# Moving rows and outputs of the split matmuls run from the last column to the first

## The chip, the cores and the metric

The kernel runs on one core of one Trainium2 chip. The metric is the time of one execution on the device in microseconds (us); runs before and after are compared by their medians. On this kernel a difference of less than about 0.2% can't be told from none.

## The reference

Two transformer-like blocks follow each other on 256 tokens of width 1024, all in f32. What matters here is that nearly all the work is matrix products of the tokens with weights:

```python
# first block
h = rms_norm(x, norm_mix);  z = h @ w_in              # 1024 -> 7000
#   recurrent branch, gated linear attention, attention over a memory of 256 rows
proj = jnp.einsum("bsnc,ncd->bsnd", branches, w_branch)   # 3 x 768 -> 1024
x = x + jnp.sum(sigmoid(z_gate) * proj, axis=2) @ w_out
up = causal_dwconv(rms_norm(x, norm_ffn) @ w_up, ...)      # 1024 -> 6144
x = x + (gelu(gate_h) * val_h) @ w_down                    # 3072 -> 1024
# second block, on rms_norm(x, final_norm)
u = rmsnorm(x, norm_mix) @ w_in_2                      # attention, state space and pooling mixers
x = x + concat(y_attn, y_ssd, y_pool) @ w_out_2
x = x + (silu(gate) * up) @ w_down_2                   # up, gate: 1024 -> 5632; 2816 -> 1024
return rmsnorm(x, norm_final_2)
```

## The kernel before, in words

**Precision.** An f32 operand is split into two parts, high (`wh`, `xh`) and low (`wl`, `xl`), of type float32r, which TensorE multiplies in one pass. `mm3` makes a product out of three matmuls into the same PSUM tile: high by high (L194), high by low (L195), low by high (L196). Each of them is a weight load (the stationary operand, 128 columns) and a stream of the moving operand (one row in each partition, 256 columns or so) through the array into PSUM.

**Weights.** They come from HBM in the order of `wplan`, a chunk of 1 MB a transfer, three half chunks ahead. ScalarE rounds a half chunk to `wh` (L149), VectorE takes the rest to `wl` (L150). The whole program is written out in this order, with no loop on the chip; element-wise work of other stages is put between the chunks.

**Which operand is stationary.** `chunk_T` (and `down_T`, `last_T` for the first down projection) makes an output that is transposed: weights are stationary, activations (256 tokens) move. A chunk has 256 output columns, which are two tiles of 128; in HBM the columns of the two tiles stand in turn, so a tile's weights are every second float:

```python
c = slice(m, m + nm * (P - 1) + 1, nm)      # chunk_T: nm = 2 tiles, the m-th one
c = (mo // 2) * 2 * P + mo % 2              # pair_cols, for down_T and last_T
return slice(c, c + 2 * P - 1, 2)
```

`chunk_tok` makes an output with tokens in partitions: activations are stationary (128 adjacent columns), weights move (256 columns; 262 or 272 for two chunks). `down_tok` and `last_tok`, the second down projection, do the same with 512 moving columns. Other matmuls with weights in adjacent columns are the 84 of `rg_gate`, the 24 of the narrow chunk xbc3, and the 24 of the scores against the memory.

**Order at the start of a sum.** For the first chunk behind a normalization (wout0, up0, gu0) `chunk_T` is called with `lo_last`: the products with the low part of the activations come last, from L223, since that part is ready last.

Plain f32 matmuls (transposes, the state-space mixer, softmax products) call `pe.matmul` or `pe.transpose` by themselves and not through `mm3`.

Of the kernel before, what the change touches and what calls it, by code (L numbers as in the profile page):

```python
# [17 lines left out]
P = 128  # L18
# [90 lines left out]
def build(ctx: ExitStack, tc: tile.TileContext, ins: dict, out: bass.AP):  # L109
    nc = tc.nc  # L110
    act, dve, pool, pe = nc.scalar, nc.vector, nc.gpsimd, nc.tensor
# [18 lines left out]
    def t2(shape=None, dt=F32):  # L130
        return tp.tile(shape or [P, 512], dt, tag="t2", name=uid("t2"))
# [8 lines left out]
    def bank(shape=None):  # L140
        return psp.tile(shape or [P, 2, 256], F32, tag="ps", name=uid("ps"))
# [45 lines left out]
    def load_w(name, i):  # L187
        q = halves.index((name, i))
        while nxt[0] < min(q + AHEAD + 1, len(halves)):
            emit_half()  # L190
        return loaded.pop((name, i))

    def mm3(o, lh, ll, rh, rl, start, stop, skip=False):
        pe.matmul(o, lh, rh, start=start, stop=False, skip_group_check=skip)  # L194
        pe.matmul(o, lh, rl, start=False, stop=False, skip_group_check=skip)  # L195
        pe.matmul(o, ll, rh, start=False, stop=stop, skip_group_check=skip)  # L196
# [6 lines left out]
    def chunk_T(name, x, nk=KT, nm=2, k_outer=False, lo_last=False):  # L203
        ps = bank()
        for i in range(2):
            wh, wl = load_w(name, i)
            od = [(m, k) for m in range(nm) for k in range(nk // 2)]
            if k_outer:
                od.sort(key=lambda q: q[1])
            for m, k in od:  # L210
                c = slice(m, m + nm * (P - 1) + 1, nm)
                kk = i * (nk // 2) + k
                if lo_last:
                    pe.matmul(ps[:, m, :], wh[:, k, c], x[0][:, kk, :], start=kk == 0 and m == 0,  # L214
                              stop=False, skip_group_check=True)
                    pe.matmul(ps[:, m, :], wl[:, k, c], x[0][:, kk, :], start=False, stop=False,  # L216
                              skip_group_check=True)
                else:
                    mm3(ps[:, m, :], wh[:, k, c], wl[:, k, c], x[0][:, kk, :], x[1][:, kk, :],
                        kk == 0 and m == 0, kk == nk - 1, skip=True)  # L220
            for m, k in od if lo_last else ():
                kk = i * (nk // 2) + k
                pe.matmul(ps[:, m, :], wh[:, k, m:m + nm * (P - 1) + 1:nm], x[1][:, kk, :], start=False,  # L223
                          stop=kk == nk - 1, skip_group_check=True)
        return ps

    def chunk_tok(name, x, nk=KT, wide=False, k_outer=False):

        pss = [bank([P, 512]) for _ in range(2)] if wide else None
        ps = None if wide else bank()  # L230
        for i in range(2):
            wh, wl = load_w(name, i)
            n = wh.shape[2]
            od = [(t, k) for t in range(2) for k in range(nk // 2)]
            if k_outer:
                od.sort(key=lambda q: q[1])
            for t, k in od:
                c = slice(t * P, (t + 1) * P)
                kk = i * (nk // 2) + k
                o = pss[t][:, :n] if wide else ps[:, t, :]  # L240
                mm3(o, x[0][:, kk, c], x[1][:, kk, c], wh[:, k, :], wl[:, k, :],
                    kk == 0 and (wide or t == 0), kk == nk - 1, skip=True)
        return pss if wide else ps
# [94 lines left out]
    m = (mh, ml)  # L338
# [10 lines left out]
    for q in range(4):  # L349
        mem_part(q)  # L350
        for n, name in enumerate(first):
            if q == 0:
                raws[name] = wrp.tile([P, WMAX], F32, tag="raw", name=uid("raw"))
            if q % 2 == 0:
                fw[n] = (whp.tile([P, WMAX // 2], F32R, tag="wh", name=uid("wh")),
                         wlp.tile([P, WMAX // 2], F32R, tag="wl", name=uid("wl")))
            o = WOFF[name][0]
            cr = slice(512 * q, 512 * q + 512)
            c = slice(512 * (q % 2), 512 * (q % 2) + 512)
            nc.sync.dma_start(raws[name][:, cr],  # L360
                              W[o:o + P * 2048].rearrange("(p n) -> p n", p=P)[:, cr])
            split(fw[n][0][:, c], fw[n][1][:, c], raws[name][:, cr])
            for k in range(2):
                for mo in range(2):
                    w0 = c.start + k * 256 + mo
                    cw = slice(w0, w0 + 2 * P - 1, 2)
                    kk = 2 * q + k
                    mm3(fps[n][:, mo, :], fw[n][0][:, cw], fw[n][1][:, cw],
                        mh[:, kk, :], ml[:, kk, :], kk == 0 and mo == 0, kk == KT - 1, skip=True)
# [24 lines left out]

    x_part(0)
    c2 = chunk_T("memk2", m)
    rm = widen(rm_tok, "nA")

# [126 lines left out]
    for j in range(3):  # L525
        ps = chunk_T(f"mq{j}", h)
        if j == 0:
            rx = widen(rx_tok, "nB")
        evac_hl(mq, j, ps, rx)
# [14 lines left out]
    for j in range(3):  # L544
        ps = chunk_T(f"zrnn{j}", h)
        evac_T(zr[:, 2 * j:2 * j + 2, :], ps, rx)
        for f in (2 * j, 2 * j + 1):
            conv_tile(xr[:, f, :], zr[:, f, :], lambda i: pv("rnn_w", 6 * i + f), pv("rnn_b", f), 4)
            split(xrh[:, f, :], xrl[:, f, :], xr[:, f, :])
        step()  # L550
# [50 lines left out]
    for j in range(3):  # L601
        ps = chunk_T(f"qk{j}", h)
# [177 lines left out]
    for j in range(3):  # L780
        ps = chunk_tok(f"v{j}", h, wide=j == 0)
# [22 lines left out]
    for bi, b in enumerate(BR_ORDER):  # L804
# [4 lines left out]
        for j in range(4):  # L809
            ps = chunk_T(f"gate{b}_{j}", h)  # L810
# [3 lines left out]
            o = (outa, outb, outc)[b]  # L814
            ps = chunk_T(f"br{b}_{j}", o, nk=MT)
# [407 lines left out]
    for i, name in enumerate(IN2_ORDER):  # L1223
        if i == 1:
            squares(x2, [sb])
        if name.startswith("vz"):
            ps = chunk_tok(name, h2, wide=i == 0, k_outer=i == 0)
        else:
            ps = chunk_T(name, h2, nm=1 if name == "xbc3" else 2)
# [97 lines left out]
    for t in range(2):  # L1327
        ssq = small([P, 2])
        o = [t2(), t2()]
# [17 lines left out]
        else:  # L1347
            act.activation(o[0], o[0], AF.Copy, scale=r)
            nc.scalar.dma_start(out[rows, 0:512], o[0])
            for i in range(2):  # L1350
                c = slice(256 * i, 256 * i + 256)
# [148 lines left out]
```

## Time and profile before

| | |
|---|---|
| median of 3 runs | 827.11 us (827.09 to 827.94) |
| the profiled execution | 826.78 us, of which 825.0 us are its span, from the first instruction to the last |
| TensorE, matmuls | 814.7 us busy (99%), 6454 instructions |
| TensorE, weight loads | 790.5 us busy (96%), 6454 instructions |
| VectorE | 606.2 us busy (73%) |
| ScalarE | 474.5 us busy (58%) |
| GpSimd | 64.4 us busy (8%) |
| DMA | 144 MB, 175 GB/s on the mean |

Matmuls overlap in TensorE's pipeline, so the busy time says only that TensorE never stood still. What one matmul costs is the distance from its start to the start of the next one.

### The profile page before, as it was taken

How to read it: one execution, taken by the hardware profiler on the slowest of the kernel's cores; microseconds unless marked ns; L12 is line 12 of the kernel's file. 1: busy time of each engine (PE TensorE's matmuls, PEld its weight loads, DVE VectorE, ACT ScalarE, POOL GpSimd, SP SyncE). 2: the span in 40 equal slices, each digit the busy share in tenths (PEclk: the TensorE clock that was granted, in tenths of full speed). 3: DMA queues.
4: the chain of work that ended last, by engine and by line, in shares of the span. 5: the costliest groups of instructions: out<-in, count | busy, mean ns of one | idle time of the engine just before them, and what ended most of it. 6: DMA issues, size and time to landing. Idle time of an engine off the chain costs nothing. (4 is left out here: it accounts for less than half of the span.)

```text
span 825.0 us, 15638 instructions
## 1 busy us (share of the span) xinstructions
PE 814.7 (99%) x6454; PEld 790.5 (96%) x6454; DVE 606.2 (73%) x950; ACT 474.5 (58%) x756; POOL 64.4 (8%) x69
## 2 busy tenths in 40 slices
PE   8999999999999999999999999999999999999996
PEld 8999999999999999999999999999999999999995
DVE  6888757866667677898777787798988756655663
ACT  6845579953445555765555555766966544444443
POOL 2210110000010002000000000207302000000000
PEclk9999999999999999999999999999999999999999
DMA  7774444354345554365555454362163554555521
GB/s 239 292 256 147 167 135 179 124 198 167 129 152 199 195 196 166 126 234 199 172 185 192 168 203 165 116 259 104 60 244 133 215 189 165 196 188 174 201 103 51
DMA packets 23527, 144.04 MB, mean 175 GB/s; under 512 B 2896, under 2 KB 3424, under 8 KB 8480
## 3 DMA queue, kind: packets, MB, share of 16 engines
q1 hardware_dynamic: 22464, 140.98, 48.1%
q0 software_dynamic: 704, 1.80, 0.6%
q8 instruction: 50, 0.82, 0.4%
q10 hardware_dynamic: 288, 0.27, 0.1%
q14 instruction: 21, 0.17, 0.1%
HBM read 141.20 MB, written 1.05 MB: 172 GB/s over the span
## 5 line engine op out<-in xcount | busy, mean ns | idle before, releaser
L150 DVE TENSOR_TENSOR wl<-raw,wh 128x1024 fp32r<-128x1024 f32 (+4 forms) x276 | 329.6, 1201 | 131.6 <-ACT wh L149 128.8
L149 ACT ACTIVATE wh<-raw 128x1024 fp32r<-128x1024 f32 (+4 forms) x276 | 278.5, 1015 | 240.2 <-PE ps L195 182.4
L194 PE MATMUL ps<-H,wh 128*128 128x256 f32 x1320 | 373.7, 283 | 1.4 <-ACT wh L149 1.4
L196 PE MATMUL ps<-H,wl 128*128 128x256 f32 x1320 | 373.7, 283 | 0.2 <-DVE wl L150 0.2
L195 PE MATMUL ps<-H,wh 128*128 128x256 f32 x1320 | 373.1, 283 | 0.0
L194 PEld LDWEIGHTS ps<-H,wh 128*128 128x128 f32 x1320 | 257.5, 195 | 3.7 <-issue 1.6
L195 PEld LDWEIGHTS ps<-H,wh 128*128 128x128 f32 x1320 | 257.0, 195 | 0.3
L196 PEld LDWEIGHTS ps<-H,wl 128*128 128x128 f32 x1320 | 256.3, 194 | 0.4 <-DVE wl L150 0.4
L196 PE MATMUL aux<-S,wl 128*128 128x256 f32 x192 | 54.3, 283 | 0.0
L195 PE MATMUL aux<-S,wh 128*128 128x256 f32 x192 | 54.3, 283 | 0.0
L194 PE MATMUL ps<-wh,H 128*128 128x256 f32 (+2 forms) x192 | 54.2, 282 | 0.0
L196 PE MATMUL ps<-wh,H 128*128 128x256 f32 (+2 forms) x192 | 53.8, 280 | 0.0
L195 PE MATMUL ps<-wl,H 128*128 128x256 f32 (+2 forms) x192 | 53.8, 280 | 0.0
L194 PE MATMUL aux<-S,wh 128*128 128x256 f32 x192 | 53.8, 280 | 0.0
L149 ACT ACTIVATE S<-t 128x256 fp32r<-128x256 f32 x46 | 19.0, 415 | 49.2 <-DVE t L919 25.5
L287 POOL TENSOR_TENSOR t<-t,t 128x512 f32<-128x512 f32 x15 | 21.7, 1448 | 325.6 <-DVE H L153 199.8
L541 DVE SCALAR_TENSOR_TENSOR t<-t,par,t 128x255 f32<-128x255 f32 (+1 forms) x96 | 40.2, 479 | 0.1
L194 PEld LDWEIGHTS aux<-S,wh 128*128 128x128 f32 x192 | 37.4, 195 | 0.0
L195 PEld LDWEIGHTS aux<-S,wh 128*128 128x128 f32 x192 | 37.2, 194 | 0.0
L196 PEld LDWEIGHTS aux<-S,wl 128*128 128x128 f32 x192 | 37.1, 193 | 0.0
L194 PEld LDWEIGHTS ps<-wh,H 128*128 128x128 f32 x192 | 36.1, 188 | 0.4 <-issue 0.4
L196 PEld LDWEIGHTS ps<-wh,H 128*128 128x128 f32 x192 | 36.1, 188 | 0.2
(332 smaller groups left out, 1132.8 us busy)
## 6 DMA issues: line engine op xcount, KB each, us to landing
raw<-w SPq DMA_DIRECT2D x115, 1024.0 KB, 4.8
raw<-w SPq DMA_DIRECT2D x12, 768.0 KB, 4.2
raw<-w SPq DMA_DIRECT2D x12, 256.0 KB, 5.4
raw<-w SPq DMA_DIRECT2D x2, 896.0 KB, 4.5
raw<-w SPq DMA_DIRECT2D x1, 1088.0 KB, 5.0
raw<-w SPq DMA_DIRECT2D x1, 1048.0 KB, 4.8
R<-memT SPq DMA_DIRECT2D x4, 256.0 KB, 5.5
R<-xT SPq DMA_DIRECT2D x2, 512.0 KB, 9.0
```

What stands on the lines that cost most here:

```text
L149: act.activation(dst_h, src, AF.Copy)
L150: dve.tensor_tensor(dst_l, src, dst_h.bitcast(F32), op=ALU.subtract)
L194: pe.matmul(o, lh, rh, start=start, stop=False, skip_group_check=skip)
L195: pe.matmul(o, lh, rl, start=False, stop=False, skip_group_check=skip)
L196: pe.matmul(o, ll, rh, start=False, stop=stop, skip_group_check=skip)
L287: self.eng.tensor_tensor(self.acc, self.acc, sq, op=ALU.add)
L541: dve.scalar_tensor_tensor(dst[:, s:], src[:, :S - s], w(width - 1 - s), dst[:, s:], op0=ALU.mult, op1=ALU.add)
```

## The change

`mm3` and the three matmuls of `chunk_T` that don't go through it read the moving row with step -1 from the last column, and write the output with step -1 from the last column. Output column j is still made from moving column j, so each value lands where it did. Weights, their layout and their loads are the same.

```diff
     def mm3(o, lh, ll, rh, rl, start, stop, skip=False):
+
+        o, rh, rl = (t[:, ::-1] for t in (o, rh, rl))
         pe.matmul(o, lh, rh, start=start, stop=False, skip_group_check=skip)
         pe.matmul(o, lh, rl, start=False, stop=False, skip_group_check=skip)
         pe.matmul(o, ll, rh, start=False, stop=stop, skip_group_check=skip)
...
                 if lo_last:
-                    pe.matmul(ps[:, m, :], wh[:, k, c], x[0][:, kk, :], start=kk == 0 and m == 0,
+                    o, xm = ps[:, m, ::-1], x[0][:, kk, ::-1]
+                    pe.matmul(o, wh[:, k, c], xm, start=kk == 0 and m == 0,
                               stop=False, skip_group_check=True)
-                    pe.matmul(ps[:, m, :], wl[:, k, c], x[0][:, kk, :], start=False, stop=False,
-                              skip_group_check=True)
+                    pe.matmul(o, wl[:, k, c], xm, start=False, stop=False, skip_group_check=True)
...
             for m, k in od if lo_last else ():
                 kk = i * (nk // 2) + k
-                pe.matmul(ps[:, m, :], wh[:, k, m:m + nm * (P - 1) + 1:nm], x[1][:, kk, :], start=False,
+                pe.matmul(ps[:, m, ::-1], wh[:, k, m:m + nm * (P - 1) + 1:nm], x[1][:, kk, ::-1], start=False,
                           stop=kk == nk - 1, skip_group_check=True)
```

All five engines have the same instructions in the same order before and after. In the compiled program a matmul's moving row before has start 0 and step 1, after start 255 and step -1, and so has its output (511 for the wide ones). The weight load of a `chunk_T` tile starts at the tile's last column and has step -2 (two floats), before and after; one with adjacent columns has step -1.

## Rows read from the trace of the kernel before

**Rows 1.** The head of the page: span; busy time, share and instructions of each engine; the granted clock of TensorE in 40 slices, in tenths.

```profile
span 825.0 us, 15638 instructions
PE 814.7 (99%) x6454; PEld 790.5 (96%) x6454; DVE 606.2 (73%) x950; ACT 474.5 (58%) x756; POOL 64.4 (8%) x69
PEclk9999999999999999999999999999999999999999
```

**Rows 2.** The chain of work that ended last, by engine and line, as shares of the span.

```profile
PE 27%; DVE 1%; ACT 0%; issue 0%; DVEq 0%; ACTq 0%
PE ps L196 6%; PE ps L194 6%; PE ps L195 6%; PE aux L196 2%; PE aux L194 2%; PE aux L195 2%; PE ps L223 0%; PE ps L216 0%; PE ps L214 0%; PE aux L1287 0%; PE aux L1017 0%; DVE V L994 0%; DVE V L995 0%; PE aux L1003 0%; DVE t L1203 0%; PE aux L1218 0%
```

**Rows 3.** All waits of TensorE: line waited for, us in total, times, the longest.

```profile
PE ps L194 <- ACT wh L149: 1.4, 1, 1.4
PE aux L1003 <- ACT t L1109: 1.1, 1, 1.1
PE wps L254 <- DVE ones L247: 1.0, 1, 1.0
PE aux L1058 <- DVE V L978: 0.2, 1, 0.2
PE ps L196 <- DVE wl L150: 0.2, 1, 0.2
```

**Rows 4.** Groups of matmuls by line and shape: out<-in by name, rows * weight columns, output shape, count, then busy us and mean ns of one, then idle time before. L519 is plain f32.

```profile
L195 PE MATMUL ps<-H,wh 128*128 128x256 f32 x1320 | 373.1, 283 | 0.0
...
L196 PE MATMUL ps<-wh,H 128*128 128x256 f32 x160 | 44.4, 278 | 0.0
...
L194 PE MATMUL aux<-wh,S 128*128 128x512 f32 x88 | 34.6, 393 | 0.0
...
L519 PE MATMUL aux<-t,M 128*128 128x256 f32 x16 | 4.1, 392 | 0.0
```

**Rows 5.** Timeline of TensorE's matmuls in the first feed-forward (`chunk_T`): start us, duration us.

```profile
300.36 0.28 PE L194 MATMUL ps<-H,wh 128*128 128x256 f32 x1
300.48 0.28 PE L195 MATMUL ps<-H,wh 128*128 128x256 f32 x1
300.60 0.28 PE L196 MATMUL ps<-H,wl 128*128 128x256 f32 x1
300.72 0.28 PE L194 MATMUL ps<-H,wh 128*128 128x256 f32 x1
...
301.08 0.28 PE L194 MATMUL ps<-H,wh 128*128 128x256 f32 x1
...
301.44 0.28 PE L194 MATMUL ps<-H,wh 128*128 128x256 f32 x1
...
301.80 0.28 PE L194 MATMUL ps<-H,wh 128*128 128x256 f32 x1
```

**Rows 6.** Busy time of each engine (and instructions that touch the stretch) in two stretches, the first feed-forward and the wide matmuls at the end: stretch, its length, then PE, PEld, DVE, ACT, POOL, the granted clock, DMA share, GB/s.

```profile
360.00:500.00 140.00, 140.00 (x1169) 140.00 (x1168) 109.99 (x166) 77.32 (x115) 0.00 (x0) 1.00 0.55 194
...
802.00:818.00 16.00, 16.00 (x72) 13.13 (x71) 7.02 (x15) 6.58 (x13) 0.00 (x0) 1.00 0.08 30
```

**Rows 7.** Timeline of matmuls of the memory's values (`chunk_tok`), start and duration in us.

```profile
37.75 0.28 PE L195 MATMUL ps<-wl,H 128*128 128x256 f32 x1
...
38.34 0.28 PE L194 MATMUL ps<-wh,H 128*128 128x256 f32 x1
38.45 0.34 PE L195 MATMUL ps<-wl,H 128*128 128x256 f32 x1
38.63 0.28 PE L196 MATMUL ps<-wh,H 128*128 128x256 f32 x1
...
39.53 0.28 PE L195 MATMUL ps<-wl,H 128*128 128x256 f32 x1
```

**Rows 8.** Timeline of weight loads (PEld) at the start of the kernel, every second float: start and duration in us; in brackets the idle time before and what ended it.

```profile
6.96 0.19 PEld L194 LDWEIGHTS ps<-H,wh 128*128 128x128 f32 x1 [1.58 <-ACT wh L149]
7.08 0.20 PEld L195 LDWEIGHTS ps<-H,wh 128*128 128x128 f32 x1
7.69 0.19 PEld L196 LDWEIGHTS ps<-H,wl 128*128 128x128 f32 x1 [0.42 <-DVE wl L150]
7.80 0.20 PEld L194 LDWEIGHTS ps<-H,wh 128*128 128x128 f32 x1
```

**Rows 9.** The same around the sum of squares, L294, whose four loads have 128 adjacent columns and whose matmuls have one moving column; the loads from 44.17 on are of `chunk_T`.

```profile
43.73 0.53 PEld L294 LDWEIGHTS aux<-ones,t 128*128 128x128 f32 x4
44.17 0.20 PEld L194 LDWEIGHTS ps<-H,wh 128*128 128x128 f32 x1
44.30 0.20 PEld L195 LDWEIGHTS ps<-H,wh 128*128 128x128 f32 x1
```

**Rows 10.** Groups of weight loads: the first is of `chunk_T` (every second float, but for the few of xbc3), the second of `chunk_tok` (adjacent columns); busy us, mean ns of one.

```profile
L195 PEld LDWEIGHTS ps<-H,wh 128*128 128x128 f32 x1320 | 257.0, 195 | 0.3
...
L195 PEld LDWEIGHTS ps<-wl,H 128*128 128x128 f32 x192 | 36.1, 188 | 0.0
```

## The prediction

> **What bounds the kernel now.** I read the page's head first, then the chain of work that ended last, then the waits of TensorE, and only then single matmuls. TensorE is busy for 814.7 of the 825.0 us and its granted clock is 9 or more tenths in every slice, the upper of its two levels, 2.4 GHz [rows 1]. The named lines of the chain are nearly all matmuls of `mm3`, L194 to L196 [rows 2]. All that TensorE waited for is 4.8 us [rows 3]. So no engine feeds it late; the kernel lasts as long as its matmuls, one behind the other, and the question is what one matmul costs from its start to the next one's start. The duration in the groups (283 ns, [rows 4]) doesn't tell that, since matmuls overlap in the pipeline. The timeline does.
>
> In `chunk_T` and `down_T` (weights as the stationary operand, every second float of a half chunk) a group of three starts every 0.36 us: 300.36, 300.72, 301.08, 301.44, 301.80 [rows 5]. That is 0.120 us a matmul, and in 140 us of the first feed-forward there are 1169 of them; less the two that only reach into the stretch from its edges, 140 / 1167 = 0.120 us [rows 6]. There VectorE is busy for 110 of the 140 us.
>
> In `chunk_tok` the activations are stationary, with their columns side by side. There the spacing is 0.118 us up to 38.34 (37.75 to 38.34 is five starts), and 0.113 us behind one longer step (38.63 to 39.53 is eight), with code, tiles and shapes unchanged [rows 7]. The wide matmuls of the last stage (512 columns) need 16 us / 70 = 0.229 us each [rows 6].
>
> What sets the 0.120? Two things run in parallel: the stream of matmul i, and the weight load for matmul i+1. So I looked for weight loads beside which no long stream runs. At 6.96 us TensorE starts behind an idle stretch of 1.58 us; the load that follows, whose own matmul can't stream before its weights are in, starts 0.12 us later; at 7.69, the same again, 0.11 [rows 8]. At 44.17 the matmuls ahead have one column; the next load starts 0.13 us later [rows 9]. So a load of every second float takes 0.11 to 0.13 us by itself, 0.12 on the mean. Four loads with adjacent columns, on the same one-column matmuls, take 44.17 - 43.73 = 0.44 us, 0.110 each [rows 9]. The recorded loads differ by about as much, 195 against 188 ns [rows 10]. I conclude that in `chunk_T` the weight load is what a matmul waits for: 0.120 us with every second float, 0.113 with adjacent ones at best.
>
> How long is the stream itself? Bounded from above by 0.113 us (256 columns in the better stretch of rows 7, where load and stream both fit), and from the wide matmuls, whose load is covered twice over, by 0.229 / 2 = 0.115 us. So under the 0.120 of `chunk_T` the stream has 5 to 7 ns of slack.
>
> **The change part by part.** No instruction is added, removed or moved on any engine, and no wait, tile or transfer changes; weights and their loads are as before. 6084 matmuls get two other patterns, step -1 for the moving row and for the output. By the code 5088 of them have every second float as weights: 12 chunks of 48 for memk, mq, zrnn and qk, 12 of 48 for the gates, 12 of 36 for the branches, 4 of 48 for wout, 24 for up, 12 for dn, 7 for the second layer's projections, 4 for wo2, 22 for gu. Then 264 are wide (three groups of 88, of which rows 4 show one), and 732 have adjacent weight columns and 256 to 272 moving ones.
>
> The trace of before has no backward stream and no backward write, so the price is bounded from both sides.
>
> - The 5088: if a backward stream takes what a forward one takes, it stays under the load, and the change costs 0. The cover is 5 to 7 ns a matmul; gone past it, each further nanosecond costs 5.1 us. From below: the stream can't shorten a step that the load sets, except for what the stream adds to the load. Against the quickest load of rows 8, 0.11, that would be up to 7 ns. I take 0, since the mean of the three loads without a stream is the 0.120 itself.
> - The 264 wide ones: here the stream sets the step. From above, twice the half-rate price below; from below, 0.229 can fall to twice the 0.113 of a short one less one step's overhead, some 0.22: 264 x 0.01 = 2.6 us gained. I take 0.
> - The 732: load and stream are nearly equal, and the step jumps between 0.113 and 0.118 without a change of code [rows 7]. All of them changing sides would be 732 x 0.0045 = 3.3 us either way; about half stand on each side now, so I keep 1.6 us for the range and take 0.
>
> Sum: 0 + 0 + 0. The profiled execution took 826.78 us, 1.8 more than its span, and the median of the runs shown is 827.11, 0.3 above it. The forecast is **827.1 us, no change**, with 1 to 3 us either way from the last two terms. Within 0.2% (1.7 us) is what a measurement of this kernel can't tell from no change.
>
> The Trainium skill, TensorE: Matmul & The Clock Gate, section LDWEIGHTS (loading the stationary operand), gives columns / 1.2 ns for a load, which is 107 ns for 128 columns, whatever their step. The trace disagrees a little: it has 110 for adjacent columns and 120 for every second float, and the measured ones stand in the sum. By the Trainium skill's figure load and stream would be equal in all 5820 narrow matmuls and there would be no slack of 5 to 7 ns.
>
> **The rivals.**
>
> *Faster: the two streams get out of each other's way.* In the compiled program a weight load starts at the last column and goes back, by two floats in `chunk_T`; before, the moving row comes towards it, and after, both go back over 1024 bytes in the same time. If reads of the two hinder each other when they meet, going the same way would end it. For it: the jump from 0.118 to 0.113 on unchanged code [rows 7] is what a hindrance that hangs on relative timing would look like. Against it: the loads without a stream beside them already take 0.12 [rows 8, 9], which leaves the hindrance 0 to 7 ns. Price: from 0.120 to 0.117 or, at the far end, 0.113: 5088 x 0.003 = 15 us or 5088 x 0.007 = 36 us, the middle of it 802 us. VectorE at 110 of 140 us has room for that. The Trainium skill, TensorE: Matmul & The Clock Gate, section Step-by-step, says that weights and moving rows have read ports of their own, so that the next load takes nothing from the running matmul; by that this rival would be worth 0.
>
> *Much slower: a backward pattern is not streamed at the full rate.* If pairs of neighbouring columns are fetched or written together only in rising order, a backward stream runs at half rate. The nearest rows are plain f32 matmuls with 256 columns, 392 ns against 283 ns [rows 4], 0.109 more. Then the stream passes the load by far: 5820 x 0.109 = 634 us and 264 x 0.218 = 58 us, about 1520 us. It decides as soon as a stream needs over 5 to 7 ns more than now. Against it: the weight loads step backward too, and keep 0.110 with adjacent columns [rows 9], but they take a column in 0.9 ns and not in 0.45, so they don't exclude it. The Trainium skill, SBUF — State Buffer, section Door 1: The DMA port swizzle, says that any PSUM access pattern that isn't contiguous slows matmuls significantly, as its lines there are 8 bytes; whether step -1 counts as contiguous it doesn't say, and every pair from column 255 down does share such a line. The same section of the Trainium skill says that SBUF bears steps of up to four floats for free. The trace has 0.120 against 0.113 for a step of two, so I don't lean on it.
>
> *A little slower: the backward stream is longer by some per cent.* At 10% more it would be 0.126, 6 ns past the load: 5088 x 0.006 + 732 x 0.011 + 264 x 0.023 = 45 us, 872 us. At 5% only the last two terms count, 4 + 3 us, 834 us. No row speaks for it.
>
> **How the numbers follow.** No change of the step in `chunk_T`: 0.53, of which 0.40 within 0.2%, 0.07 faster and 0.06 slower by the two smaller terms. Streams out of each other's way: 0.24. Half rate: 0.13. Some per cent longer: 0.10. So faster 0.07 + 0.24 = 0.31, same 0.40, slower 0.06 + 0.13 + 0.10 = 0.29. The range leaves out the half rate, the upper half of the last case and the far end of the faster one: 795 to 842 us, about 0.78. The likeliest case alone has 824 to 830.
>
> **What the profile of the changed kernel would show.** If I am right, groups of three in the feed-forward still start every 0.36 us, the stretch 360 to 500 us again holds about 1169 matmuls, and the span is 825 us. If the first rival holds, the starts stand 0.35 us or less apart, while loads without a stream still take 0.12. If the second holds, the step is near 0.22 us, the recorded matmul near 390 ns, and VectorE's share falls by half. The wide matmuls tell it best: only there is the stream alone on the path, so a step that leaves 0.229 prices the backward stream itself. I am wrong if the recorded load is not what holds the next matmul up, that is if those three early loads were long for a reason of their own.

## The result and the profile after

The changed kernel takes 819.43 us (819.26 to 819.52), before it was 827.11. The ratio is 0.9904, 95% interval 0.9881 to 0.9926: 7.7 us or 1.0% faster, five times what can be told from no change. The forecast, 827.1 us and no change as the likeliest case, did not come. The time lies inside the stated range of 795 to 842 us, which had been drawn wide enough for the milder part of the first rival. What that rival had named, shorter steps among the 5088 matmuls with every second float, is what came, at less than its smallest price of 15 us.

The head of the page after, beside [rows 1]:

```profile
span 817.7 us, 15648 instructions
...
PE 807.2 (99%) x6454; PEld 781.6 (96%) x6454; DVE 605.3 (74%) x950; ACT 474.2 (58%) x756; POOL 63.8 (8%) x69
```

The span is 7.3 us shorter and TensorE's matmuls 7.5 us; the other engines' busy time moved by less than 1 us, and TensorE is still busy 99% of the time. So the whole difference is in the steps from one matmul to the next.

Timeline of matmuls in the first feed-forward after the change (start and duration in us), as in [rows 5]; `mm3` is now on L196 to L198:

```profile
300.08 0.28 PE L196 MATMUL ps<-H,wh 128*128 128x256 f32 x1
...
300.43 0.28 PE L196 MATMUL ps<-H,wh 128*128 128x256 f32 x1
...
303.26 0.28 PE L196 MATMUL ps<-H,wh 128*128 128x256 f32 x1
```

Busy time of each engine in 360 to 500 us after, columns as in [rows 6]:

```profile
360.00:500.00 140.00, 140.00 (x1191) 140.00 (x1190) 110.83 (x167) 79.56 (x116) 0.00 (x0) 1.00 0.55 193
```

From 300.08 to 303.26 there are 27 steps: 0.1178 us each, where it was 0.1200. The stretch of 140 us holds 1191 matmuls instead of 1169; less the two at its edges, 140 / 1189 = 0.1177. The recorded duration, 0.28, didn't move at all. 5088 matmuls by 2.2 ns are 11.2 us, more than the kernel gained.

The rest was lost again in the matmuls with adjacent weight columns. Timeline of `chunk_tok` after, the memory's values, beside [rows 7], and then of the wide matmuls at the end:

```profile
37.39 0.28 PE L196 MATMUL ps<-wh,H 128*128 128x256 f32 x1
...
39.55 0.28 PE L196 MATMUL ps<-wh,H 128*128 128x256 f32 x1
...
794.78 0.40 PE L198 MATMUL aux<-wh,S 128*128 128x512 f32 x1
795.02 0.40 PE L196 MATMUL aux<-wh,S 128*128 128x512 f32 x1
...
799.92 0.40 PE L196 MATMUL aux<-wh,S 128*128 128x512 f32 x1
```

`chunk_tok` goes at (39.55 - 37.39) / 18 = 0.120 us, where it was 0.118 and 0.113. The wide ones go at (799.92 - 794.78) / 22 = 0.2336, where it was 0.229. Added up over all start-to-start distances in the two traces, the 5088 with every second float went from 615.2 to 604.2 us (-11.0), the 636 adjacent ones with 256 columns from 78.1 to 80.4 (+2.3), and the wide ones from 60.4 to 61.5 (+1.1). Together -7.6, against the 7.3 of the span.

### The profile page after: what moved, and what is told of

It is laid out like the page before. It is cut to its first block, busy times and chain, and to the rows that moved or that the text cites. A ratio compares the mean times of both kernels' runs of the same rounds, so it can differ in the third digit from the quotient of the medians.

```text
span 817.7 us, 15648 instructions
## 1 busy us (share of the span) xinstructions
PE 807.2 (99%) x6454; PEld 781.6 (96%) x6454; DVE 605.3 (74%) x950; ACT 474.2 (58%) x756; POOL 63.8 (8%) x69
## 5 line engine op out<-in xcount | busy, mean ns | idle before, releaser
L196 PE MATMUL ps<-H,wh 128*128 128x256 f32 x1320 | 374.8, 284 | 1.4 <-ACT wh L149 1.4
L198 PE MATMUL ps<-H,wl 128*128 128x256 f32 x1320 | 372.8, 282 | 0.2 <-DVE wl L150 0.2
L196 PEld LDWEIGHTS ps<-H,wh 128*128 128x128 f32 x1320 | 255.6, 194 | 3.9 <-ACT wh L149 1.7
L198 PEld LDWEIGHTS ps<-H,wl 128*128 128x128 f32 x1320 | 255.6, 194 | 0.4 <-DVE wl L150 0.4
L196 PE MATMUL ps<-wh,H 128*128 128x256 f32 (+2 forms) x192 | 54.9, 286 | 0.0
L198 PE MATMUL ps<-wh,H 128*128 128x256 f32 (+2 forms) x192 | 54.6, 284 | 0.0
L196 PE MATMUL aux<-S,wh 128*128 128x256 f32 x192 | 54.1, 282 | 0.0
L198 PE MATMUL aux<-S,wl 128*128 128x256 f32 x192 | 54.1, 282 | 0.0
L289 POOL TENSOR_TENSOR t<-t,t 128x512 f32<-128x512 f32 x15 | 21.4, 1426 | 320.6 <-DVE H L153 196.1
L196 PEld LDWEIGHTS aux<-S,wh 128*128 128x128 f32 x192 | 37.1, 193 | 0.0
L198 PEld LDWEIGHTS aux<-S,wl 128*128 128x128 f32 x192 | 37.1, 193 | 0.0
L196 PEld LDWEIGHTS ps<-wh,H 128*128 128x128 f32 x192 | 36.1, 188 | 0.4 <-issue 0.4
L198 PEld LDWEIGHTS ps<-wh,H 128*128 128x128 f32 x192 | 36.1, 188 | 0.2
```

Source lines behind the costliest of these rows:

```text
L289: self.eng.tensor_tensor(self.acc, self.acc, sq, op=ALU.add)
```

## The experiments

The theories, after the result. **A**: what a matmul costs beside its load hangs on the order in which the moving row is read. **B**: on the order in which the output is written. For what comes on top: the load alone (its layout) or the two reads together.

**Reads alone, writes alone.** Each kernel has one half of the change. Below is the line of `mm3` against the changed kernel, with the new line of the one kernel and of the other; the three matmuls of `chunk_T` that don't go through `mm3` are changed in the same way.

```diff
-        o, rh, rl = (t[:, ::-1] for t in (o, rh, rl))
+        rh, rl = (t[:, ::-1] for t in (rh, rl))      # the one
+        o = o[:, ::-1]                               # the other
...
```

> Only the moving rows are read backward; outputs are written forward, so the tokens (or columns) of the products stand in reversed order and the output's values differ; the work is the same. Theory A (the weight load's read and the moving row's read hinder each other when they run towards one another): the reads are as in the changed kernel, so the step in the first feed-forward is 0.1178 us and the time 819 us. Theory B (the order of the writes to PSUM is what shortened the step): step 0.120 us as before, 827 us.

> Only the outputs are written backward; moving rows are read forward, so the products stand in reversed order and the output's values differ; the work is the same. Theory A (reads): step 0.120 us as before, 827 us. Theory B (writes): 0.1178 us, 819 us.

Reads backward: 819.33 us, ratio 0.990 (0.9883 to 0.9917), all of the gain. Writes backward: 828.02 us, ratio 0.9999 (0.9989 to 1.0008), nothing. The stretch 360 to 500 us of the one and of the other:

```profile
360.00:500.00 140.00, 140.00 (x1191) 140.00 (x1190) 110.75 (x167) 79.49 (x116) 0.00 (x0) 1.00 0.56 193
```

```profile
360.00:500.00 140.00, 140.00 (x1169) 140.00 (x1168) 110.59 (x169) 78.27 (x115) 0.00 (x0) 1.00 0.54 191
```

1191 matmuls as after, and 1169 as before. B falls; writing a PSUM row from its last column costs nothing here (828.02 against 827.98 us of the kernel before in the same runs).

**Weights in adjacent columns.** The kernel before, and the changed one, with the two tiles of a half chunk side by side instead of in turn (the layout in HBM changes with it).

```diff
...
-                c = slice(m, m + nm * (P - 1) + 1, nm)
+                c = slice(m * P, (m + 1) * P)
...
-        v = in_turn(ch[n]) if stationary(n) and b % 256 == 0 else ch[n]
+        v = ch[n]
```

> The kernel before with the columns of each weight tile adjacent, not in turn with those of the other tile; rows forward. Theory A says that a step is the load alone (0.110 us for adjacent columns) plus 3 ns, plus what the two reads hinder each other: 0.1133 us as in the better stretch of the chunk_tok matmuls, or 0.1177 as in the worse one, so 5088 x 0.0067 or 0.0023 us less: 793 to 815 us. Rival: the step of 0.120 is no matter of the load but of the 256 columns and their writes: 827 us.

> The changed kernel with adjacent weight columns: both reads go backward, the moving row at twice the bytes a second. Theory A in its form that only equal speed in the same direction keeps the reads apart: step 0.120 us, as the chunk_tok matmuls of the changed kernel have it (0.1200 against 0.1133 to 0.1177 before), about 830 us. Rival: going the same way is what helps, whatever the speeds: 0.1133 us or less, 793 us.

With rows forward 806.89 us, ratio 0.9744 (0.9729 to 0.9758): 21 us under the kernel before in the same runs (827.98) and 12.5 under the changed one, the best of all kernels here. That is inside the 793 to 815 that theory A gave, and the rival, by which the layout of the weights doesn't matter, falls. With rows backward 820.04 us, ratio 0.9906 (0.9891 to 0.9921), where I had expected neither. Two stretches of the first, and one of the second:

```profile
250.00:300.00 50.00, 50.00 (x444) 50.00 (x442) 38.15 (x47) 28.07 (x37) 0.16 (x1) 1.00 0.60 207
360.00:500.00 140.00, 140.00 (x1191) 140.00 (x1191) 110.29 (x170) 80.17 (x118) 0.00 (x0) 1.00 0.54 189
```

```profile
360.00:500.00 140.00, 140.00 (x1191) 140.00 (x1190) 110.73 (x168) 79.38 (x116) 0.00 (x0) 1.00 0.56 194
```

Forward, the step is 50 / 442 = 0.113 us in one stretch and 140 / 1189 = 0.1177 in another, with the same code, tiles and shapes. It is the jump of [rows 7] again, now in `chunk_T`. The trace holds one of the two over tens of microseconds and changes at an interruption (a plain f32 product, a pause). Backward, the step is never 0.113 but 0.1177 throughout in this stretch, and 0.120 in `chunk_tok` and in a few of the last chunks. So reading backward is no gain by itself. With adjacent columns it costs about 13 us (806.9 to 820.0), and with every second float it gains 8 to 9.

**Backward for every second float alone.** All calls of `mm3` with adjacent weight columns read and write forward again, but for the scores against the memory. (By the trace the scores are 48 matmuls, 24 of 128 rows and 24 of 64, where the text on the kernel names 24; the count of 732 holds all 48.)

```diff
-    def mm3(o, lh, ll, rh, rl, start, stop, skip=False):
+    def mm3(o, lh, ll, rh, rl, start, stop, skip=False, back=True):
+        if back:
+            o, rh, rl = (t[:, ::-1] for t in (o, rh, rl))
...
-                    kk == 0 and (wide or t == 0), kk == nk - 1, skip=True)
+                    kk == 0 and (wide or t == 0), kk == nk - 1, skip=True, back=False)
...
```

> The changed kernel, but backward only where the weights are every second float (5088 matmuls); the 732 narrow matmuls with adjacent weight columns (less the 24 of the scores, which stay backward) and the 264 wide ones read forward as before. If the time is the sum of steps, the two groups give back what they lost in the changed kernel, 2.3 and 1.1 us: 816 us. Rival: the steps of the groups hang on one another (by the state that one leaves to the next), and it stays at 819 us.

818.47 us (817.55 to 819.40), ratio 0.9884 (0.9866 to 0.9901). By the start-to-start distances, the 5088 took 604.3 us as after, the adjacent ones 79.4 and the wide ones 61.4. The last is 1.0 us more than the 60.4 before, although these matmuls read forward as before. So of the 3.4 us that the adjacent and wide ones lost, only about 1 came back. The time is nearer to the 819 of the rival, by which the steps of the groups hang on one another, than to the 816 of the plain sum.

The wide matmuls of this run show it. Timeline, two rows of each of the first two runs of 24, the last row of a run among them, start and duration in us:

```profile
660.29 0.39 PE L197 MATMUL aux<-wh,S 128*128 128x512 f32 x1
...
663.50 0.39 PE L199 MATMUL aux<-wh,S 128*128 128x512 f32 x1
...
675.04 0.40 PE L197 MATMUL aux<-wh,S 128*128 128x512 f32 x1
...
680.41 0.40 PE L199 MATMUL aux<-wh,S 128*128 128x512 f32 x1
```

The first 24 stand behind plain f32 products and go at (663.50 - 660.29) / 14 = 0.229 us. The next 24, the same code, stand directly behind narrow matmuls that read backward and go at (680.41 - 675.04) / 23 = 0.2335, and so do all later ones. So the direction alone doesn't decide: a run of matmuls can take over a step from what stood before it.

**The load by itself.** Blocks of 48 matmuls of one form ahead of the kernel before, one line of code each, among them streams that read the same one element 256 times, beside which the load has nobody to share with.

```diff
+    _ = [pe.matmul(pp_[:, 0:256], pw[:, 0:128], pm[:, 0:1].to_broadcast([P, 256]), ...) for a, b in r48]
+    _ = [pe.matmul(pp_[:, 0:256], pw[:, 0:256:2], pm[:, 0:1].to_broadcast([P, 256]), ...) for a, b in r48]
...
```

> The kernel before with 28 blocks of 48 matmuls ahead of its work, each block one weight tile and one moving row over and over, on data in SBUF, with no other engine busy: weights adjacent, every second and every fourth float; moving rows of 64 to 512 columns, forward, backward, or one element again and again. Theory L (in the kernel before the weight load was what each matmul waited for): with 64 columns the step is the load's own, 0.113 us adjacent and 0.120 with every second float, and with 256 columns it is no longer, whatever the direction. Theory H (the two reads cost each other time): with 64 columns, and with 256 of one element, steps stand at 0.107 to 0.114 us for both layouts, and only 256 different columns forward with every second float give 0.120; backward gives 0.118.

Timeline, one row a block: start, duration, line, shape, count. The step is the distance to the next block's start over 48. L267 and L270 have every second float and 256 moving columns, forward and back; L268 has every fourth float as weights and 256 moving columns. L276 (adjacent) and L277 (every second float) have the one-element stream. L278 to L282 have 512 columns: adjacent forward, adjacent back, every second float forward, the same back, and one element. L289 has 128 columns and every second float, forward.

```profile
44.74 5.92 PE L267 MATMUL ps<-S,S 128*128 128x256 f32 x48
50.49 11.37 PE L268 MATMUL ps<-S,S 128*128 128x256 f32 x48
61.70 5.85 PE L269 MATMUL ps<-S,S 128*128 128x256 f32 x48
67.38 5.92 PE L270 MATMUL ps<-S,S 128*128 128x256 f32 x48
73.14 11.36 PE L271 MATMUL ps<-S,S 128*128 128x256 f32 x48
...
109.88 5.54 PE L276 MATMUL ps<-S,S 128*128 128x256 f32 x48
115.26 5.82 PE L277 MATMUL ps<-S,S 128*128 128x256 f32 x48
120.91 11.07 PE L278 MATMUL ps<-S,S 128*128 128x512 f32 x48
131.82 11.37 PE L279 MATMUL ps<-S,S 128*128 128x512 f32 x48
143.02 11.35 PE L280 MATMUL ps<-S,S 128*128 128x512 f32 x48
...
165.42 10.66 PE L282 MATMUL ps<-S,S 128*128 128x512 f32 x48
175.92 8.48 PE L283 MATMUL ps<-S,S 128*128 128x384 f32 x48
...
220.31 5.82 PE L289 MATMUL ps<-S,S 128*128 128x128 f32 x48
225.97 5.87 PE L290 MATMUL ps<-S,S 128*128 128x128 f32 x48
```

A load of every second float, with a stream that is no hindrance, comes round every 5.65 / 48 = 117.7 ns (L277), and with 128 real columns every 5.66 / 48 = 117.9 (L289). With adjacent columns it is 5.38 / 48 = 112.1 (L276). So the 0.1178 us of `chunk_T` after the change is as long as the load alone, and the 0.1200 before it was the load and 2.2 ns of something else. Neither theory came out as written: the load is 2.2 ns shorter than L had it, and longer than the 0.107 to 0.114 of H. The 512 columns show the same from the other side. Reading one element they take 10.50 / 48 = 218.8 ns, forward with adjacent weights 10.91 / 48 = 227.3, backward 11.20 / 48 = 233.3, and forward with every second float 233.3 as well (L280 to L281 is 11.20 by the start of L281 at 154.22). There the load is covered twice over, and its layout still moves the step: the two reads cost each other something.

In these blocks, however, 256 columns with every second float went at 120 forward and backward alike (L267, 5.75 / 48 = 119.8; L270, 5.76 / 48 = 120.0), where the kernel has 120.0 and 117.8. One thing that differed was where the tiles lie. In the compiled kernel, before and after, the weight tiles begin 128 bytes behind a multiple of 256 bytes and the activations 64 bytes behind one; in the blocks both begin at 64.

**The place of the two reads.** 24 more blocks: 16 of four forms, each with the weights moved by 0, 16, 32 and 48 floats against the row (the shift), and 8 with the order of tiles as in `mm3`, the same four forms at shift 16 (L281 to L284) and 0 (L285 to L288). Shift 16, 64 bytes, is the kernel's place in `chunk_T`; `chunk_tok`, with the roles changed, has 48, counted modulo 256 bytes.

```diff
+    _ = [pe.matmul(pq, pw[:, 16:272:2], pm[:, 0:256], ...) for a, b in r48]
+    _ = [pe.matmul(pq, pw[:, 16:272:2], pm[:, 255::-1], ...) for a, b in r48]
...
```

> 240 matmuls of 512 columns and then 24 blocks of 48 matmuls each stand ahead of the kernel before, so its time is some 200 us longer and says nothing; the step of each block is what counts. Blocks on L265 to L280 use one weight tile and one moving row over and over: every second float forward, every second float back, adjacent forward, adjacent back, each with the weight tile moved up by 0, 16, 32 and 48 floats against the moving row. Blocks on L281 to L288 go through two weight tiles and two moving rows as mm3 does, at the shift 16 and at 0. Theory P, what a matmul costs beside its load hangs on where the two reads stand in their lines of memory: within each of the four groups of four blocks the step moves between 117.8 and 120 ns (every second float) and between 113 and 120 ns (adjacent), at least one shift has 117.8 for every second float read forward, and the blocks in the manner of mm3 follow the shift alone. Theory S, the sequence of tiles decides: within each group of four all steps are alike (120 for every second float), and in L281 to L288 backward every second float comes to 117.8 where forward it is 120, at both shifts. If the direction itself counts only together with the place, backward and forward change sides at some shift.

Timeline, one row a block. L265 and L266 are every second float forward at 0 and 16; L269 and L270 the same back; L273 and L274 adjacent forward at 0 and 16:

```profile
59.77 5.92 PE L265 MATMUL ps<-S,S 128*128 128x256 f32 x48
65.52 5.93 PE L266 MATMUL ps<-S,S 128*128 128x256 f32 x48
...
82.86 5.92 PE L269 MATMUL ps<-S,S 128*128 128x256 f32 x48
88.62 5.82 PE L270 MATMUL ps<-S,S 128*128 128x256 f32 x48
94.27 5.82 PE L271 MATMUL ps<-S,S 128*128 128x256 f32 x48
...
105.58 5.92 PE L273 MATMUL ps<-S,S 128*128 128x256 f32 x48
111.33 5.62 PE L274 MATMUL ps<-S,S 128*128 128x256 f32 x48
116.80 5.85 PE L275 MATMUL ps<-S,S 128*128 128x256 f32 x48
...
150.98 5.93 PE L281 MATMUL ps<-S,S 128*128 128x256 f32 x48
156.75 5.82 PE L282 MATMUL ps<-S,S 128*128 128x256 f32 x48
162.40 5.61 PE L283 MATMUL ps<-S,S 128*128 128x256 f32 x48
167.84 5.82 PE L284 MATMUL ps<-S,S 128*128 128x256 f32 x48
173.50 5.92 PE L285 MATMUL ps<-S,S 128*128 128x256 f32 x48
179.26 5.93 PE L286 MATMUL ps<-S,S 128*128 128x256 f32 x48
185.03 5.91 PE L287 MATMUL ps<-S,S 128*128 128x256 f32 x48
```

The steps of the first 16 blocks, start to start over 48, in ns:

| shift of the weights, floats | 0 | 16 | 32 | 48 |
|---|---|---|---|---|
| every second float, forward | 119.8 | 120.0 | 121.0 | 120.2 |
| every second float, back | 120.0 | 117.7 | 117.7 | 117.9 |
| adjacent, forward | 119.8 | 114.0 | 118.5 | 117.7 |
| adjacent, back | 118.3 | 117.9 | 119.8 | 119.8 |

The column for 16 is what the kernels have in `chunk_T`: 120.0 before, 117.7 after, 113.3 or 117.7 with adjacent columns (114.0 here holds the slow first ones; the last 40 go at 113.3), 117.9 with adjacent ones back. The last field of the column for 48 is the 0.120 of `chunk_tok` after. The blocks in the manner of `mm3` have 120.2, 117.7, 113.3 and 117.9 at shift 16 (L281 to L284) and 120.0 and 120.2 at 0 (L285, L286): at both shifts they do what one tile over and over does there, so the sequence of tiles doesn't decide. One part of theory P missed: forward, no shift brought every second float to 117.8.

**The kernel at another place.** To take it from blocks to the kernel: the changed kernel, with everything behind the weight tiles in memory moved up by 64 bytes, which is shift 0.

```diff
+    gap = cp.tile([P, 16], F32, name="gap")
+    act.activation(gap[:, 0:1], ones[:, 0:1], AF.Identity)
     cst = cp.tile([P, NCST], F32, name="cst")
```

> The changed kernel, with one unused tile of 64 bytes (and one short activation that fills it) ahead of the tiles that hold the moving rows: these move up by 64 bytes, the weight tiles stay, so both now begin at the same place of a 256-byte line, where they stood 64 bytes apart. Matmuls, order and directions are those of the changed kernel. Theory P, the price of the two reads hangs on their place: the backward step of the every-second-float matmuls goes from 117.8 back to the 120.0 that the blocks at shift 0 showed, 5088 x 2.2 ns = 11 us, the adjacent ones go from 120.0 to about 118.4, 1 us less, and the time is 828 to 831 us: nothing is left of the gain. Rival, the direction alone decides in the kernel and the blocks were a case of their own: 819.4 us within 1 us.

829.56 us, ratio to the kernel before 1.0023 (1.0013 to 1.0032), in the expected 828 to 831 and 10 us above the changed kernel. The stretch 360 to 500 us:

```profile
360.00:500.00 140.00, 140.00 (x1169) 140.00 (x1168) 110.57 (x169) 78.62 (x115) 0.00 (x0) 1.00 0.54 190
```

1169 matmuls as before the change. The direction and, but for one short activation, everything else of the program is that of the changed kernel; 64 bytes take all of the gain away. The rival, by which the direction alone decides, falls. The change is good only where the tiles happen to lie.

**More places for adjacent columns.** To see whether a place gives 113.3 each time: 32 blocks in the manner of `mm3`, eight shifts, four times each in four orders.

> 32 blocks of 48 matmuls, adjacent weight columns, rows forward, in the manner of mm3, ahead of the kernel before: eight places of the weight tile against the moving row (0 to 224 bytes in steps of 32), each four times in four orders. What counts is the step of each block. If the place alone decides, the four blocks of a place agree within 0.5 ns, and one or more places have 113.3 each time. If each block's start throws the dice anew, the four of a place differ, by the same sizes 113.3, 117.8 and 120 as seen before, and only their odds hang on the place. A place that has 113.3 four times is the one to give the kernel with adjacent columns, where 806.9 us would then go towards 795.

Start to start over 48, in ns: at 0 bytes 120 four times; at 32 bytes 118.3 four times; at 64 bytes 117.7, 113.8, 117.9, 113.5; at 96 bytes 117.5, 117.3, 117.3, 118.8; at 128 bytes 118.5 to 118.8; at 160 bytes 119.8 to 120.0; at 192 bytes 117.7, 117.7, 117.9, 113.5; at 224 bytes 117.7, 116.7, 116.7, 116.5. Three of these blocks, on timeline rows with the one behind each (L271 and L290 at 192 bytes, L273 at 64):

```profile
94.31 5.81 PE L271 MATMUL ps<-S,S 128*128 128x256 f32 x48
99.96 5.82 PE L272 MATMUL ps<-S,S 128*128 128x256 f32 x48
105.61 5.62 PE L273 MATMUL ps<-S,S 128*128 128x256 f32 x48
111.07 5.92 PE L274 MATMUL ps<-S,S 128*128 128x256 f32 x48
...
201.86 5.61 PE L290 MATMUL ps<-S,S 128*128 128x256 f32 x48
207.31 5.92 PE L291 MATMUL ps<-S,S 128*128 128x256 f32 x48
```

L273 takes 5.46 us for 48, L290 5.45, and L271, at the place of L290, 5.65. So both ideas hold in part: six places keep one step within 1.5 ns, four of them within 0.5, and at the two others each start of a block fell on about 113.3 or 117.7. The kernel with adjacent columns already lies at one of these two, and no place was found that would be better for it.

## Why the prediction was wrong in its likeliest time and right in its range

**The bound: right.** TensorE's steps are the time, before and after, and nothing waited for anything new: the waits of TensorE in [rows 3] add up to 3.9 us (not to the 4.8 of the prediction), and after the change to 4.0.

**The range held, and the likeliest case in it did not come.** That case was given 824 to 830 us, and no change of the step in `chunk_T` 0.53. That 819.4 lies in the range comes from the room left for the first rival, whose middle was 802, and not from the sum of three zeros. The terms measured -11.0, +1.1 and +2.3 us.

**"The weight load is what a matmul waits for": right as a floor, wrong in size, and this is the step that failed.** I read 0.12, 0.11 and 0.13 us from [rows 8, 9], took the mean, 0.12, and found it equal to the step: "the mean of the three loads without a stream is the 0.120 itself". From that I set the term of the 5088 to 0. The load alone is 117.7 ns by the blocks on one element. The term was mis-sized by 2.2 ns a matmul, 11 us. Three rows of two decimals can't tell 0.118 from 0.120. The trace keeps the starts in whole nanoseconds: the two loads of [rows 8] are 114 and 116 ns, and only the one of [rows 9], beside matmuls of one column, is 123. Their mean is 117.7, not 120, which agrees with the blocks by luck, since the three lie 9 ns apart. I had written the right bound in the sentence before ("against the quickest load of rows 8, 0.11, that would be up to 7 ns") and left it for the mean. The same rows after the change:

```profile
7.08 0.19 PEld L196 LDWEIGHTS ps<-H,wh 128*128 128x128 f32 x1 [1.70 <-ACT wh L149]
7.19 0.20 PEld L197 LDWEIGHTS ps<-H,wh 128*128 128x128 f32 x1
7.80 0.19 PEld L198 LDWEIGHTS ps<-H,wl 128*128 128x128 f32 x1 [0.41 <-DVE wl L150]
7.92 0.20 PEld L196 LDWEIGHTS ps<-H,wh 128*128 128x128 f32 x1
```

They read 0.11 and 0.12, where before it was 0.12 and 0.11 (in whole nanoseconds 114 and 115, where before it was 114 and 116): the load itself is the same.

**The stream's slack of 5 to 7 ns: not a slack.** I treated load and stream as two clocks of which the longer one counts. With adjacent columns the load alone is 112.1 ns, and a stream of 256 columns fits into 113.3, the best step seen. Yet the same two together take 113.3, 117.7 or 120.0, by where they lie and which way they go. A maximum of two fixed numbers can't give that; beside each other they cost up to 120.0 - 112.1, some 8 ns, more than the load.

**The wide matmuls: the sign was missed, +1.1 us against 0, and so was the reason.** I took 0, with a gain of up to 2.6 us as the near bound, and wrote of them that "only there is the stream alone on the path". It isn't: in the blocks with 512 columns forward the layout of the weights moves the step from 227.3 to 233.3, and in the run with `back=False` wide matmuls that read forward go at 0.2335. So a step that leaves 0.229 doesn't price the backward stream.

**The adjacent ones: +2.3 us, under the 3.3 of all changing sides, but over the 1.6 that I kept for the range.** That they change sides was foreseen; that there is a third side, 0.120, was not.

**The first rival: right in kind, priced too high, and only half its reason stands.** Its signs came as written: three starts stand 0.35 us apart, and loads alone are unchanged. The step went to 0.1178, not to 0.117 or 0.113, since the load alone takes 117.7 ns. Its story was that two reads going towards each other meet, and two going the same way don't. That is not shown: at shift 0 both directions have 120.0, and with adjacent columns the backward row is the worse one at shift 16. What the runs show is that direction and place together decide, and in the wide matmuls also what stood before. I gave it 0.24 because the loads "already take 0.12", the same misread number. The Trainium skill, TensorE: Matmul & The Clock Gate, section Step-by-step, has weights and moving rows on read ports of their own, so that one takes nothing from the other. The runs disagree with the second half: 64 bytes of place move the step by 2.2 ns in the kernel. Where the two reads meet, no run shows.

**Half rate, or a few per cent more.** Half rate did not come. The steps of the wide matmuls did grow by 2% (0.229 to 0.2336), but those that read forward at 0.2335 show that this need not be the price of the backward stream. Writing backward costs nothing (828.02 against 827.98 us of the kernel before in the same runs).

**Open.** Which part of the memory or of TensorE the two reads share; why some places fall on 113.3 at one start and on 117.7 at another; how a run of matmuls takes over a step from what stood before it. The opposite pairing, weights that are loaded from the first column on, wasn't tried: in all compiled kernels here the load starts at the tile's last column.

## What to carry to other kernels

Where TensorE goes from matmul to matmul without a wait, measure the distance of starts over tens of them, in the kernel and in a block that has the load alone; single rows of two decimals hide the 2 ns on which such a change turns. Adjacent weight columns with forward rows were worth 21 us here (806.9 us), more than any direction tried with every second float. A gain of some nanoseconds a matmul that comes with a read pattern can be gone when another tile moves by 64 bytes, so move the tiles once before you put a gain down to the direction.

## What was not expected of the hardware

- Weights of every fourth float take twice the time of every second float: 11.21 / 48 = 233.5 ns a matmul (L268 of the blocks), against 117.7 for every second float and 112.1 for adjacent ones.
- In the kernels a step with 256 columns settles on a few sizes and keeps them: three matmuls in 340, 353.3 or 360 ns, over hundreds of matmuls, up to the next interruption.
- With a moving row of 512 columns that reads one element over and over the step is shorter than with a real one: 218.8 ns against 227.3 to 233.3.
- Writing PSUM rows from the last column to the first cost nothing: 828.02 against 827.98 us.
